# A decoder block's MLP: the down projection from seven block products instead of eight

## The chip, the cores and the metric

The kernel runs on one core of one Trainium2 chip. The metric is the device time of one execution in microseconds (us). The core's engines run side by side, each with its own instruction queue that it works off in order: TensorE (PE; its weight loads are shown apart as PEld), VectorE (DVE), ScalarE (ACT), GpSimd (POOL) and SyncE (SP), which here issues the transfers from HBM.

## What is computed

```python
# x: 256 tokens of 2048 channels, float32
xn = rmsnorm(x, norm_mix_pre);  proj = xn @ w_in          # mLSTM and attention branches, gates
x = x + rmsnorm(merged @ w_out, norm_mix_post)
hn = rmsnorm(x, norm_ffn_pre)
u = square(relu(hn @ w_up))                               # w_up:   2048 x 8192
y = u @ w_down                                            # w_down: 8192 x 2048
return x + rmsnorm(y, norm_ffn_post)
```

Only the last three lines, the MLP, are touched by the change (and where some tiles lie).

## The kernel before

Every weight is streamed once from HBM in units of 128 x 2048 float32 (1.05 MB). ScalarE casts a unit to float32r (`whi`), VectorE subtracts that from it (`wlo`), each in two halves of 1024 columns (`split`, L166 and L167). Three products then make one exact one: hi by hi, hi by lo, lo by hi. `whi` and `wlo` have four half-unit buffers each, so that a half can be split when PE is through with the half four places before it. `raw` units have three buffers.

The program is a list `steps` of (units, their products, what follows). The loop at its end splits the units of step i, then issues the products of step i - 1 and its follow-up, so a split is written one step ahead of its products. A scheduler in the build then sets the final order on each engine's queue; the engines keep to it.

The MLP works in `NCH` = 8 chunks of 1024 hidden channels.

- An *up step* (8 in a chunk) makes 128 channels of u for 256 tokens from one unit of w_up. `mm_feat` issues, for each of 16 k, one matmul of 512 columns (L185: the activation's hi and lo parts side by side) and one of 256 (L186). The two halves are then added by `both` (L216 copy on ScalarE, L218 on VectorE), scaled by `rbc`, squared with the relu (`up_post`, L726, L728), and split into hi and lo by `split_act` (L223, L224) into the tile `ut`.
- A *down step* (8 in a chunk: four column blocks `e` of 512, two halves `v` of the chunk's channels) takes one unit of w_down through `mm_tok`: 4 k, 2 token halves, 3 matmuls of 512 columns (L197, L201, L202), 24 in all. After `v` = 1 the sums of the two token halves are added into `y` in SBUF (L773; for the first chunk copied by ScalarE, L771).

Up steps of chunk j + 1 and down steps of chunk j follow each other eight by eight. The last chunk ends with `down_step` for two column blocks, `hold_step` (units split ahead) and `last_step`, which also does the last norm. The output projection's last unit alone goes through `mm_feat_one` (L209 to L211), three matmuls of 256 columns into one region.

```python
for k in range(KT):                       # mm_feat_one, the three of one k
    PE.matmul(out=acc[:, 0:T], lhsT=hi, rhs=m[:, 0, :], start=k == 0, stop=False)
    PE.matmul(out=acc[:, 0:T], lhsT=hi, rhs=m[:, 1, :], start=False, stop=False)
    PE.matmul(out=acc[:, 0:T], lhsT=lo, rhs=m[:, 0, :], start=False, stop=k == KT - 1)
```

Of the kernel before, what the change touches and what calls it, by code (L numbers as in the profile page):

```python
# [23 lines left out]
P = 128  # L24
# [8 lines left out]
# columns of the groups of av and the gates, and where they start  # L33
# [22 lines left out]
# 2 pi in three parts of 12 bits and a rest, for an exact reduction  # L56
# [29 lines left out]
def tile_hybrid_block(ctx, tc, xT, pos, pre, small, wa, wi, wo, wu, wd, wpost, out):  # L86
# [7 lines left out]
    pa = ctx.enter_context(tc.tile_pool(name="pa", bufs=1))  # L94
    pb = ctx.enter_context(ExitStack())
# [40 lines left out]
    def keep_warm(n):  # L136
        """Products that nobody reads, so that the tensor engine's clock is up."""
# [39 lines left out]
    def mm_feat(accs, units, mov, k0=0, nk=KT, after_k=None, tail=0):  # L177
        """The halves of accs[i][c, 512] sum to unit i's product; mov(k) is [128, 2, T]: hi, lo."""
# [11 lines left out]
    def mm_tok(accs, parts, mov, kbase, start, stop, halves=(0, 1), n=512):  # L190
        """accs[h][tok, n] accumulate over the unit's four k."""
# [12 lines left out]
    def mm_feat_one(acc, parts, mov):  # L204
        """acc[c, :T] is the product, in one region."""
        for k in range(KT):
            m = mov(k)
            hi, lo = wk(parts, k, P)
            PE.matmul(out=acc[:, 0:T], lhsT=hi, rhs=m[:, 0, :], start=k == 0, stop=False)  # L209
            PE.matmul(out=acc[:, 0:T], lhsT=hi, rhs=m[:, 1, :], start=False, stop=False)  # L210
            PE.matmul(out=acc[:, 0:T], lhsT=lo, rhs=m[:, 0, :], start=False, stop=k == KT - 1)  # L211

    def both(acc):
        """The two halves of mm_feat's result, added."""
# [6 lines left out]
    def split_act(dst, src, scale):  # L221
        """dst[:, 0], dst[:, 1] = hi, lo of src * scale (a number or one per partition)."""
# [4 lines left out]
    def newton(dst, y, v, n):  # L227
        """One step of dst = v ** -0.5 from y."""
# [5 lines left out]
    def rsqrt(dst, v, n):  # L234
        """dst = v ** -0.5, from the exponent's halving: no activation table is touched."""
# [8 lines left out]
    def rsqrt_act(dst, v, n):  # L244
        """dst = v ** -0.5 with a square root of the scalar engine and a step of Newton's."""
# [6 lines left out]
    def col_stats(col, sq, root):  # L252
        """col[tok, half] = rstd from the sums over channels of the arrays sq[channel, token]."""
# [11 lines left out]
    def bc_row(dst, col):  # L265
        """dst[any, tok] = col[tok]."""
# [24 lines left out]
    def rope_tables():  # L291
# [14 lines left out]
        # sin(ang) and sin(ang + pi/2), both arguments brought into [-pi, pi]  # L306
# [70 lines left out]
    def gates(pg):  # L377
# [13 lines left out]
        # log sigmoid(f) = min(f, 0) - log(1 + exp(-|f|))  # L391
# [9 lines left out]
        # with r = i - b: m - b per token (m0, and m1 - b's last sum of the first chunk; m1)  # L401
# [19 lines left out]
    def conv(cb, dst, acc):  # L421
# [11 lines left out]
        # twice silu(o) = o (1 + tanh(o / 2))  # L433
# [11 lines left out]
    def mlstm(h, qk):  # L445
# [16 lines left out]
        # q and k hold twice their values: 1/4 of that, and k's 256 ** -0.5  # L462
# [30 lines left out]
    def mlstm_out(h, hn):  # L493
        for vt in range(2):
# [5 lines left out]
            # times twice the sigmoid, 1 + tanh; the half follows  # L500
# [11 lines left out]
    def feat_step(src, mov, post, after_k=None, tail=0):  # L512
        st = {}

        def mm(units):
            st["a"] = [acc_tile() for _ in units]
            mm_feat(st["a"], units, mov, after_k=after_k, tail=tail)
# [40 lines left out]
    def gate_post(name, acc):  # L558
        s = both(acc)
        V.tensor_tensor(out=s, in0=s, in1=rbc, op=ALU.mult)  # L560
        g = pa.tile([P, T], F32, name="gt", tag="gt", bufs=8)
# [40 lines left out]
    def then(f, *args):  # L602
        """f follows the last step, after what already does."""
# [32 lines left out]
        # a head's memory is read two steps after its last unit  # L636
# [10 lines left out]
    def mix_post(c, acc):  # L647
# [6 lines left out]
        if c == 0:  # L654
            # the table of the square root, before it is waited for
# [15 lines left out]
    def residual():  # L671
        """x += mix's norm, and its operands for the MLP, in this order on the vector engine."""
# [32 lines left out]
    def open_mlp():  # L705
        """The residual by tokens."""
        pb.close()
        pool["f"] = pb.enter_context(tc.tile_pool(name="pf", bufs=1))
        x1 = late["x1"] = pa.tile([P, 2, D], F32, name="x1", tag="ha")
        late["y"] = pa.tile([P, 2, D], F32, name="y", tag="hm")  # L710
        late["wp"] = pool["f"].tile([P, D], F32, name="wp_bc")
        nc.sync.dma_start(out=late["wp"], in_=wpost.partition_broadcast(P))
        late["ssq"] = pool["f"].tile([P, 2, 4], F32, name="ssq")
        for k0 in range(0, KT, 4):
            for h in range(2):
# [4 lines left out]
                S.copy(out=x1[:, h, k0 * P:(k0 + 4) * P], in_=ps)  # L720

    ut = {}

    def up_post(j, i, acc):
        s = both(acc)
        V.tensor_tensor(out=s, in0=s, in1=rbc, op=ALU.mult)  # L726
        r = t256()
        V.scalar_tensor_tensor(out=r, in0=s, scalar=0.0, in1=s, op0=ALU.max, op1=ALU.mult)  # L728
        if i % 4 == 0:
            ut[j, i // 4] = pool["f"].tile([P, 4, 2, T], F32R, name="ut", tag="ut", bufs=4)  # L730
# [26 lines left out]

    def down_step(j, e, v):
        def mm(units):
            if v == 0:  # L760
                tok_acc["d"] = [acc_tile(), acc_tile()]
            mm_tok(tok_acc["d"], units[0], umov(j), 4 * v, v == 0, v == 1)

        def post():
            if v == 0:
                return
            y = late["y"]
            es = slice(e * 512, (e + 1) * 512)
            for h in range(2):
                if j == 0:  # L770
                    S.copy(out=y[:, h, es], in_=tok_acc["d"][h])  # L771
                elif j < NCH - 1:
                    V.tensor_tensor(out=y[:, h, es], in0=tok_acc["d"][h], in1=y[:, h, es],  # L773
                                    op=ALU.add)
                else:
                    last_sum(h, e, tok_acc["d"][h])
                    last_scale(h, e)
        steps.append(([wd[8 * j + 2 * e + v]], mm, post))

    def umov(j):  # L780
        return lambda k: ut[j, k // 4][:, k % 4]

    def last_sum(h, e, acc):
        """y's last part, and the sum of its squares."""
        y = late["y"][:, h, e * 512:(e + 1) * 512]
        add = V.tensor_tensor(out=y, in0=acc, in1=y, op=ALU.add)
        q = pool["f"].tile([P, 512], F32, name="q512", tag="q512", bufs=1)
# [3 lines left out]
    def last_scale(h, e):  # L791
        es = slice(e * 512, (e + 1) * 512)
# [3 lines left out]
    def hold_step(v):  # L796
        """A unit of the last step, split ahead of it into the place of the MLP's operands."""
# [8 lines left out]
    def last_step():  # L806
        """The last columns of y, the first tokens' before the others', and the last norm."""
        j, e = NCH - 1, 3

        def mm(units):  # L810
            units = late["held"] + units
            late["acc"] = [[acc_tile(), acc_tile()] for _ in range(2)]
            for h in range(2):
                for n in range(2):
                    for v in range(2):
                        mm_tok(late["acc"][n], units[2 * n + v], umov(j), 4 * v, v == 0, v == 1,
                               halves=(h,))

        def post():
# [3 lines left out]
            for h in range(2):  # L823
# [7 lines left out]
                yw = pool["f"].tile([P, 512], F32, name=f"yw{h}")  # L831
# [12 lines left out]
    for j in range(NCH + 1):  # L844
# [131 lines left out]
```

## Time and profile before

| | |
|---|---|
| runs shown | 1458.02, 1458.87, 1461.2 us; median 1458.87 |
| span of the profiled execution (first to last instruction) | 1456.0 us |
| that execution's own time | not listed; the median stands 2.87 us above the span |
| PE, PEld, DVE, ACT, POOL busy | 99%, 85%, 67%, 50%, 0% of the span |
| HBM read | 263.46 MB, 182 GB/s over the span |

Busy is the time in which an engine has at least one instruction in work. Matmuls are pipelined: a row's duration is longer than the distance to the next one's start, so the cost of a matmul is read from starts. An idle time is followed by what ended it. The clock row gives the granted TensorE clock in tenths of full speed.

### The profile page before, as it was taken

To read this page: it belongs to the slowest core of one execution; us is meant where nothing else is said; L and a number is where in the kernel's file an instruction comes from. 1 tells how busy PE (TensorE), PEld (TensorE's weight loads), DVE (VectorE), ACT (ScalarE), POOL (GpSimd) and SP (SyncE) were. 2 spreads that over 40 slices of the span, in tenths; PEclk is the share of its full clock that TensorE was granted. 3 is DMA by queue.
4 is the path that set the end of the run, shared out by engine and by line. 5 is a ranking of instruction groups with operands and counts; after the bars stand their busy time and mean duration, and the time that the engine had idled before them with its cause. 6 is when DMAs were issued, how large, how long until landed. Compare 5 with 4: busy or idle time off the path is not lost.

```text
span 1456.0 us, 19843 instructions
## 1 busy us (share of the span) xinstructions
PE 1444.0 (99%) x7722; PEld 1235.7 (85%) x7722; DVE 975.4 (67%) x1546; ACT 724.3 (50%) x1125; POOL 2.4 (0%) x12
## 2 busy tenths in 40 slices
PE   9999999999999999999999999999999999999997
PEld 8888888888888888888888888888888888888885
DVE  8777766686676666665778646566575665656675
ACT  7655555565554444555655444344343444434451
POOL 0000000000000000000000000000000000000000
PEclk9999999999999999999999999999999999999999
DMA  8554445555445555555634555555555555555561
GB/s 265 211 183 166 167 173 174 174 174 174 172 175 193 183 190 186 188 188 184 221 145 153 194 181 195 182 194 181 194 178 198 178 198 178 199 178 198 177 227 58
DMA packets 42141, 266.83 MB, mean 183 GB/s; under 512 B 4800, under 2 KB 7104, under 8 KB 11200
## 3 DMA queue, kind: packets, MB, share of 16 engines
q1 hardware_dynamic: 41904, 265.57, 52.4%
q8 instruction: 60, 0.98, 0.3%
q14 instruction: 33, 0.27, 0.1%
q10 hardware_dynamic: 144, 0.01, 0.0%
HBM read 263.46 MB, written 2.10 MB: 182 GB/s over the span
## 4 chain that ended last, share of the span: by engine, by line
PE 98%; ACT 1%; DVE 0%; DMA 0%; issue 0%; DVEq 0%; SPq 0%; ACTq 0%
PE acc L185 42%; PE acc L186 22%; PE acc L202 10%; PE acc L197 10%; PE acc L201 10%; PE sm L141 0%; PE sm L340 0%; ACT whi L166 0%; PE sm L457 0%; PE sm L364 0%; PE sm L447 0%; DMA raw<-in_wa_dram 0%; PE sm L359 0%; ACT x L720 0%; DVE x L839 0%
## 5 line engine op out<-in xcount | busy, mean ns | idle before, releaser
L167 DVE TENSOR_TENSOR wlo<-raw,whi 128x1024 fp32r<-128x1024 f32 (+2 forms) x504 | 599.9, 1191 | 422.6 <-ACT whi L166 412.8
L166 ACT CAST whi<-raw 128x1024 fp32r<-128x1024 f32 (+2 forms) x504 | 515.0, 1023 | 650.6 <-PE acc L185 296.6
L185 PE MATMUL acc<-xw,whi 128*128 128x512 f32 x1152 | 408.9, 395 | 0.0
L185 PE MATMUL acc<-hw,whi 128*128 128x512 f32 x992 | 349.8, 394 | 0.1
L186 PE MATMUL acc<-xw,wlo 128*128 128x256 f32 x1152 | 328.5, 285 | 0.0
L186 PE MATMUL acc<-hw,wlo 128*128 128x256 f32 x992 | 280.4, 283 | 0.0
L185 PEld LDWEIGHTS acc<-xw,whi 128*128 128x128 f32 x1152 | 216.4, 188 | 50.3 <-issue 2.1
L185 PEld LDWEIGHTS acc<-hw,whi 128*128 128x128 f32 x992 | 186.2, 188 | 43.2 <-DVE t L218 0.4
L186 PEld LDWEIGHTS acc<-xw,wlo 128*128 128x128 f32 x1152 | 216.7, 188 | 0.9
L202 PE MATMUL acc<-wlo,ut 128*128 128x512 f32 x496 | 197.6, 398 | 0.0
L201 PE MATMUL acc<-whi,ut 128*128 128x512 f32 x496 | 195.3, 394 | 0.0
L197 PE MATMUL acc<-whi,ut 128*128 128x512 f32 x496 | 194.9, 393 | 0.0
L186 PEld LDWEIGHTS acc<-hw,wlo 128*128 128x128 f32 x992 | 186.5, 188 | 0.4
L201 PEld LDWEIGHTS acc<-whi,ut 128*128 128x128 f32 x496 | 93.1, 188 | 23.6
L197 PEld LDWEIGHTS acc<-whi,ut 128*128 128x128 f32 x496 | 93.1, 188 | 22.1
L202 PEld LDWEIGHTS acc<-wlo,ut 128*128 128x128 f32 x496 | 93.1, 188 | 21.8
L185 PE MATMUL acc<-mg,whi 128*128 128x512 f32 x240 | 84.2, 393 | 0.0
L218 DVE TENSOR_TENSOR t<-acc,t 128x256 f32<-128x256 f32 x183 | 75.8, 417 | 0.9 <-ACT t L216 0.9
L186 PE MATMUL acc<-mg,wlo 128*128 128x256 f32 x240 | 67.7, 283 | 0.0
L216 ACT COPY t<-acc 128x256 f32<-128x256 f32 x183 | 66.6, 366 | 0.0
L197 PE MATMUL acc<-whi,xw 128*128 128x512 f32 (+1 forms) x160 | 54.4, 356 | 0.3 <-ACT whi L166 0.3
L201 PE MATMUL acc<-whi,xw 128*128 128x512 f32 (+1 forms) x160 | 54.6, 357 | 0.0
(234 smaller groups left out, 1238.4 us busy)
## 6 DMA issues: line engine op xcount, KB each, us to landing
raw<-in_wi_dram SPq DMA_DIRECT2D x96, 1024.0 KB, 4.8
raw<-in_wu_dram SPq DMA_DIRECT2D x64, 1024.0 KB, 4.9
raw<-in_wd_dram SPq DMA_DIRECT2D x64, 1024.0 KB, 4.8
raw<-in_wo_dram SPq DMA_DIRECT2D x16, 1024.0 KB, 4.8
raw<-in_wa_dram SPq DMA_DIRECT2D x8, 520.0 KB, 4.8
raw<-in_wa_dram SPq DMA_DIRECT2D x16, 256.0 KB, 4.7
x<-in_xT_dram SPq DMA_DIRECT2D x16, 128.0 KB, 4.6
out_dram<-x SPq DMA_DIRECT2D x8, 256.0 KB, 2.7
```

What stands on the lines that cost most here:

```text
L166: S.copy(out=hi[:, s], in_=r)
L167: V.tensor_tensor(out=lo[:, s], in0=r, in1=hi[:, s].bitcast(F32), op=ALU.subtract)
L185: PE.matmul(out=accs[i][:, 0:2 * T], lhsT=hi, rhs=m, start=k == 0, stop=False)
L186: PE.matmul(out=accs[i][:, 0:T], lhsT=lo, rhs=m[:, 0, :], start=False, stop=k == nk - 1)
L197: first = PE.matmul(out=acc, lhsT=m[:, 0, ts], rhs=hi, start=start and k == 0, stop=False)
L201: PE.matmul(out=acc, lhsT=m[:, 1, ts], rhs=hi, start=False, stop=False)
L202: PE.matmul(out=acc, lhsT=m[:, 0, ts], rhs=lo, start=False, stop=stop and k == 3)
L216: S.copy(out=b, in_=acc[:, T:2 * T])
L218: V.tensor_tensor(out=s, in0=acc[:, 0:T], in1=b, op=ALU.add)
```

## The change

For chunks 0 to 6 the down projection's block products (two token halves by two column blocks, summed over two channel halves) are made by a seven-product scheme in the manner of Strassen and Winograd. With A the chunk's activations (A11, A12: first token half, channel halves 0 and 1; A21, A22: second) and B the four weight units of a pair of column blocks, the steps of a group are, in program order:

| step | activation factor | weight factor | how the weight factor is made | goes into |
|---|---|---|---|---|
| p1 | A11 | B11 | loaded | v, and on to p2's bank |
| q5 | A21 - A22 | T1 = B11 + B12 | VectorE (L856) | y22, on to q3's bank |
| p6 | q5's - A11 | T2 = T1 + B22 | VectorE (L862), in place | v |
| p2 | A12 | B21 | loaded | with p1: y11 |
| q7 | A11 - A21 | T3 = B12 + B22 | accumulating transfer from POOL (L871) onto B12 | y22, on to q4's bank |
| q3 | p6's + A12 | B22 | loaded | with q5: y12 |
| q4 | A22 | T4 = T2 + B21 | VectorE (L878), in place | with q7: y21 |

The scheme's common sum `v` is kept over all chunks and added to y12, y21, y22 at the end of chunk 6. A chunk has two groups (column blocks 0 and 1, 2 and 3), so 14 *down steps*, each of 12 matmuls (`mm_factor`). The 8 up steps of the next chunk, U0 to U7, stand among them: p1 U0 q5 U1 p6 p2 U2 q7 U3 q3 q4 U4, then p1 U5 q5 p6 U6 p2 U7 q7 q3 q4. All up steps go through `mm_feat_one`; `up_post` is one operation on VectorE (L757) and a square on ScalarE; the seven activation factors of a chunk are split once (`factor`, L773 and L774). B22 is fetched twice. The last chunk keeps its ordinary steps. Line numbers of the changed kernel: L169 and L170 are the split, L215 to L217 an up step's matmuls, L226, L230, L232 a down step's, L846 and L897 the operations into v and y. Some tiles move (`x` and the gates into a pool that is closed for the MLP, `wp_bc` into a weight buffer near the end).

```diff
-    def mm_feat_one(acc, parts, mov):
+    def mm_feat_one(accs, units, mov, after_k=None, tail=0):
...
+    def mm_factor(acc, parts, f, start, stop, pinned=False, more=False):
+        for k in range(4):
+            hi, lo = wk(parts, k, 512)
+            first = PE.matmul(out=acc, lhsT=f[:, k, 0], rhs=hi, start=start and k == 0,
+                              stop=False, skip_group_check=more)
...
+            PE.matmul(out=acc, lhsT=f[:, k, 1], rhs=hi, start=False, stop=False,
+                      skip_group_check=more)
+            PE.matmul(out=acc, lhsT=f[:, k, 0], rhs=lo, start=False, stop=stop and k == 3,
+                      skip_group_check=more)
...
     def up_post(j, i, acc):
-        s = both(acc)
-        V.tensor_tensor(out=s, in0=s, in1=rbc, op=ALU.mult)
         r = t256()
-        V.scalar_tensor_tensor(out=r, in0=s, scalar=0.0, in1=s, op0=ALU.max, op1=ALU.mult)
+        V.scalar_tensor_tensor(out=r, in0=acc[:, 0:T], scalar=0.0, in1=rbc, op0=ALU.max,
+                               op1=ALU.mult)
...
-        split_act(ut[j, i // 4][:, i % 4], r, 1.0)
+        S.activation(out=uh[c][:, i % 4], in_=r, func=AF.Square)
+        if j < NCH - 1 and i == 7:
+            todo.extend(factors(j))
+            for _ in range(4):
+                todo.pop(0)()
...
+    def factor(name, src):
+        f = xs[name] = pool["f"].tile([P, 4, 2, P], F32R, name="xs", tag="xs", bufs=7)
+        S.copy(out=f[:, :, 0], in_=src)
+        V.tensor_tensor(out=f[:, :, 1], in0=src, in1=f[:, :, 0].bitcast(F32), op=ALU.subtract)
...
+    def long_raw():
+        return pool["f"].tile([P, 2048], F32, name="rawl", tag="rawl", bufs=4)
...
+        def w_t1():
+            r["12"], r["t"] = long_raw(), long_raw()
+            nc.sync.dma_start(out=r["12"], in_=b12)
+            V.tensor_tensor(out=r["t"], in0=r["11"], in1=r["12"], op=ALU.add)
+            return [split(r["t"])]
...
+        def w_t2():
+            r["22"] = long_raw()
+            nc.sync.dma_start(out=r["22"], in_=b22)
+            V.tensor_tensor(out=r["t"], in0=r["t"], in1=r["22"], op=ALU.add)
+            return [split(r["t"])]
...
+        def w_t3():
+            nc.gpsimd.dma_start(out=r["12"], in_=b22, accum_op=ALU.add)
+            return [split(r["12"])]
...
+        def w_t4():
+            V.tensor_tensor(out=r["t"], in0=r["t"], in1=r["21"], op=ALU.add)
+            return [split(r["t"])]
...
+    for j in range(NCH - 1):
+        downs, i = down_group(j, 0) + down_group(j, 1), 0
+        for what in "DUDUDDUDUDDUDUDDUDUDDD":
+            if what == "D":
+                steps.append(downs.pop(0))
+            else:
+                up_step(j + 1, i)
+                i += 1
```

What the build makes of this order shows on VectorE's queue. First the queue of the kernel before, where the down steps of a chunk end and the next chunk's up steps begin (`wlo` is a lo part of a half unit, `y` the output's sums, `t` an up step's temporary):

```order
L773 TENSOR_TENSOR y<-acc,y 128x512 x2
L167 TENSOR_TENSOR wlo<-raw,whi 128x1024 x3
L218 TENSOR_TENSOR t_9879<-acc,t_9877 128x256
L726 TENSOR_TENSOR t_9879<-t_9879,rbc 128x256
L728 SCALAR_TENSOR_TENSOR t_9882<-t_9879 128x256
L167 TENSOR_TENSOR wlo<-raw,whi 128x1024
L224 SCALAR_TENSOR_TENSOR ut<-t_9882,ut 128x256
```

Now the change's queue at the like place, from the operation on U7's sums (first row) into the steps q7, q3, q4 and p1 (`rawl`: weight buffers of the group; `s_a`, `s_b`, `u`: activations and their combinations; `xs`: a factor's lo part):

```order
L757 SCALAR_TENSOR_TENSOR t_10288<-acc,rbc 128x256
L170 TENSOR_TENSOR wlo<-rawl,whi 128x1024 x2
L897 TENSOR_TENSOR y<-y,acc 128x512
L784 TENSOR_TENSOR s_a<-u 128x512
L170 TENSOR_TENSOR wlo<-rawl,whi 128x1024
L170 TENSOR_TENSOR wlo<-raw,whi 128x1024
L846 TENSOR_TENSOR y<-y,acc 128x512
L789 TENSOR_TENSOR s_b<-s_a,u 128x512
L793 TENSOR_TENSOR u<-u 128x4x128
L170 TENSOR_TENSOR wlo<-raw,whi 128x1024
L774 TENSOR_TENSOR xs<-s_a,xs 128x4x128
```

Between the lo parts there now stand operations into y and on activation factors. Two up steps further on, from the operation on U1's sums (first row) to the lo parts of U2 and q7, the queue of the change is:

```order
L757 SCALAR_TENSOR_TENSOR t_10558<-acc,rbc 128x256
L170 TENSOR_TENSOR wlo<-rawl,whi 128x1024 x3
L878 TENSOR_TENSOR rawl<-rawl 128x2048
L170 TENSOR_TENSOR wlo<-raw,whi 128x1024
L846 TENSOR_TENSOR v<-v,acc 128x512
L170 TENSOR_TENSOR wlo<-raw,whi 128x1024
L170 TENSOR_TENSOR wlo<-rawl,whi 128x1024
```

The sum T4 (L878) stands ahead of U2's first lo part (the single L170 behind it). On PE's queue at the same place, the end of p2 (`acc_10395`) and the start of U2 (`acc_10617`) read:

```order
L232 MATMUL acc_10395<-wlo_10568,xs_10304 128x512
L226 MATMUL acc_10395<-whi_10567,xs_10304 128x512
L230 MATMUL acc_10395<-whi_10567,xs_10304 128x512
L232 MATMUL acc_10395<-wlo_10568,xs_10304 128x512
L226 MATMUL acc_10679<-whi_10609,xs_10330 128x512
L230 MATMUL acc_10679<-whi_10609,xs_10330 128x512
L217 MATMUL acc_10617<-hw_7141,wlo_10588 128x256
```

Two hi products of q7 (`acc_10679`), and further ahead two of U2, stand before U2's first lo product (L217).

## Rows read from the trace of the kernel before

**Rows 1.** Page, part 1 (busy us, share, instructions), part 2's clock

```profile
PE 1444.0 (99%) x7722; PEld 1235.7 (85%) x7722; DVE 975.4 (67%) x1546; ACT 724.3 (50%) x1125; POOL 2.4 (0%) x12
...
PEclk9999999999999999999999999999999999999999
```

**Rows 2.** Page, part 4: the chain that ended last, by engine and by line

```profile
PE 98%; ACT 1%; DVE 0%; DMA 0%; issue 0%; DVEq 0%; SPq 0%; ACTq 0%
PE acc L185 42%; PE acc L186 22%; PE acc L202 10%; PE acc L197 10%; PE acc L201 10%; PE sm L141 0%; PE sm L340 0%; ACT whi L166 0%; PE sm L457 0%; PE sm L364 0%; PE sm L447 0%; DMA raw<-in_wa_dram 0%; PE sm L359 0%; ACT x L720 0%; DVE x L839 0%
```

**Rows 3.** Windows: length; busy PE, PEld, DVE, ACT, POOL; clock; DMA share; GB/s

```profile
1100.00:1200.00 100.00, 100.00 (x494) 83.69 (x493) 62.48 (x78) 41.74 (x52) 0.00 (x0) 1.00 0.54 187
1400.00:1456.00 56.00, 46.53 (x200) 37.10 (x198) 34.72 (x53) 17.71 (x30) 0.00 (x0) 0.96 0.35 129
```

**Rows 4.** Line L197 (down products), its instructions from 818 and 1086 us

```profile
L197 PE MATMUL acc<-whi,ut x1: 400/400/400, 818.4 to 818.4; 128*128 128x512 f32 x1
...
L197 PE MATMUL acc<-whi,ut x3: 388/392/392, 1087.6 to 1089.0; 128*128 128x512 f32 x3
```

**Rows 5.** Timeline of PE, a stretch of down products (start us, us)

```profile
818.66 0.39 PE L201 MATMUL acc<-whi,ut 128*128 128x512 f32 x1
...
848.07 0.39 PE L201 MATMUL acc<-whi,ut 128*128 128x512 f32 x1
```

**Rows 6.** Timeline of PE, a stretch of up products

```profile
800.04 0.28 PE L186 MATMUL acc<-hw,wlo 128*128 128x256 f32 x1
...
818.30 0.28 PE L186 MATMUL acc<-hw,wlo 128*128 128x256 f32 x1
```

**Rows 7.** Timeline of PE, the output projection's last unit

```profile
709.25 0.28 PE L211 MATMUL acc<-mg,wlo 128*128 128x256 f32 x1
...
714.59 0.28 PE L211 MATMUL acc<-mg,wlo 128*128 128x256 f32 x1
```

**Rows 8.** Groups of VectorE by form (busy us, mean ns | idle before)

```profile
L167 DVE TENSOR_TENSOR wlo<-raw,whi 128x1024 fp32r<-128x1024 f32 x472 | 578.1, 1225 | 419.7 <-ACT whi L166 410.1 <-PE acc L186 7.8
...
L773 DVE TENSOR_TENSOR y<-acc,y 128x512 f32<-128x512 f32 x48 | 33.1, 691 | 0.7
L728 DVE SCALAR_TENSOR_TENSOR t<-t 128x256 f32<-128x256 f32 x64 | 27.2, 425 | 2.1
...
L167 DVE TENSOR_TENSOR wlo<-raw,whi 128x512 fp32r<-128x512 f32 x16 | 11.0, 688 | 1.6 <-ACT whi L166 1.6
```

**Rows 9.** Timeline of VectorE, at three places (xN: N merged)

```profile
736.17 1.22 DVE L167 TENSOR_TENSOR wlo<-raw,whi 128x1024 fp32r<-128x1024 f32 x1
737.30 0.47 DVE L688 SCALAR_TENSOR_TENSOR hw<-x,sm_in,hw 128x256 fp32r<-128x256 f32 x1
...
1019.77 1.39 DVE L773 TENSOR_TENSOR y<-acc,y 128x512 f32<-128x512 f32 x2
...
1426.14 1.28 DVE L794 TENSOR_TENSOR y<-y,wp_bc 128x512 f32<-128x512 f32 x2
```

**Rows 10.** Groups of ScalarE by line and form

```profile
L166 ACT CAST whi<-raw 128x1024 fp32r<-128x1024 f32 x472 | 495.6, 1050 | 640.4 <-PE acc L185 296.6 <-PE acc L201 189.8 <-issue 139.4
...
L788 ACT ACTIVATE q<-y 128x512 f32<-128x512 f32 x8 | 5.1, 633 | 18.4 <-DVE y L786 18.3
```

**Rows 11.** Timelines of ScalarE and VectorE, one half unit's split

```profile
1023.03 1.05 ACT L166 CAST whi<-raw 128x1024 fp32r<-128x1024 f32 x1 [1.75 <-PE acc L201]
...
1024.12 1.23 DVE L167 TENSOR_TENSOR wlo<-raw,whi 128x1024 fp32r<-128x1024 f32 x1 [1.57 <-ACT whi L166]
```

**Rows 12.** Waits, longest first (us in total, times, longest us)

```profile
DVE wlo L167 <- ACT whi L166: 412.8, 410, 3.8
ACT whi L166 <- PE acc L185: 296.6, 217, 4.9
```

**Rows 13.** Page, part 2 (GB/s by slice) and part 6 (KB, us to landing)

```profile
GB/s 265 211 183 166 167 173 174 174 174 174 172 175 193 183 190 186 188 188 184 221 145 153 194 181 195 182 194 181 194 178 198 178 198 178 199 178 198 177 227 58
...
raw<-in_wd_dram SPq DMA_DIRECT2D x64, 1024.0 KB, 4.8
```

More of the change, by code (lines that the diff above doesn't have):

```diff
@@ L729, in up_post @@
         if i % 4 == 0:
[L730 to L731 removed]
+            uh[c] = pool["f"].tile([P, 4, T], F32, name="u", tag="u", bufs=2)
+        S.activation(out=uh[c][:, i % 4], in_=r, func=AF.Square)
[3 more added lines that the diff above has]
+                todo.pop(0)()
+        elif j == NCH - 1 and i % 4 == 3:
+            for h in range(2):
+                factor((j, c, h), uh[c][:, :, h * P:(h + 1) * P])
@@ L756, in hmov, with wd_unit, group, add @@
         return late["hw"][:, k]
+    def wd_unit(j, e, v):
+        return wd[8 * j + 2 * e + v]
+    def long_raw():
+        return pool["f"].tile([P, 2048], F32, name="rawl", tag="rawl", bufs=4)
+    def group(j, p):
+        e1, e2 = 2 * p, 2 * p + 1
+        b11, b12, b21, b22 = (wd_unit(j, e, v) for v in range(2) for e in (e1, e2))
+        y, v = late["y"], late["v"][:, p]
+        y11, y12, y21, y22 = (y[:, h, e * 512:(e + 1) * 512] for h in range(2) for e in (e1, e2))
+        r, acc = {}, {}
+        def add(dst, a, op=ALU.add):
+            if j == 0 and op == ALU.add and id(dst) not in seen:
+                seen.add(id(dst))
+                S.copy(out=dst, in_=a)
+            else:
+                V.tensor_tensor(out=dst, in0=dst, in1=a, op=op)
+        seen = set()
+        def w_b11():
+            r["11"] = load(b11)
+            return [split(r["11"])]
+        def w_t1():
[8 more added lines that the diff above has]
+            return [split(r["t"])]
+        def w_b21():
+            r["21"] = long_raw()
+            nc.sync.dma_start(out=r["21"], in_=b21)
+            return [split(r["21"])]
+        def w_t3():
+            nc.gpsimd.dma_start(out=r["12"], in_=b22, accum_op=ALU.add)
+            return [split(r["12"])]
+        def w_b22():
+            return [split(r["22"])]
+        def w_t4():
+            V.tensor_tensor(out=r["t"], in0=r["t"], in1=r["21"], op=ALU.add)
+            return [split(r["t"])]
+        def step(name, w, bank, start, post):
+            def mm(units):
+                if start:
+                    acc[bank] = acc_tile()
+                mm_factor(acc[bank], units[0], xs[j, name], start, True, more=not start)
+            def after():
+                post(acc[bank])
+                if todo:
+                    todo.pop(0)()
+                if j == NCH - 2 and name == "q4":
+                    for dst, op in ((y12, ALU.subtract), (y21, ALU.add), (y22, ALU.subtract)):
+                        V.tensor_tensor(out=dst, in0=dst, in1=v, op=op)
+            return w, mm, after
+        def q7(a):
+            V.tensor_tensor(out=y22, in0=y22, in1=a, op=ALU.subtract)
+        return [step("p1", w_b11, "a", True, lambda a: add(v, a)),
+                step("q5", w_t1, "e", True, lambda a: add(y22, a)),
+                step("p6", w_t2, "f", True, lambda a: add(v, a)),
+                step("p2", w_b21, "a", False, lambda a: add(y11, a)),
+                step("q7", w_t3, "b", True, q7),
+                step("q3", w_b22, "e", False, lambda a: add(y12, a)),
+                step("q4", w_t4, "b", False, lambda a: add(y21, a))]
@@ L761, in mm @@
                 tok_acc["d"] = [acc_tile(), acc_tile()]
-            mm_tok(tok_acc["d"], units[0], umov(j), 4 * v, v == 0, v == 1)
+            for h in range(2):
+                mm_factor(tok_acc["d"][h], units[0], xs[j, v, h], v == 0, v == 1)
         def post():
[L765 to L775, printed above, removed]
+            if v == 1:
+                for h in range(2):
                     last_sum(h, e, tok_acc["d"][h])
                     last_scale(h, e)
-        steps.append(([wd[8 * j + 2 * e + v]], mm, post))
-    def umov(j):
-        return lambda k: ut[j, k // 4][:, k % 4]
+        steps.append(([wd_unit(j, e, v)], mm, post))
     def last_sum(h, e, acc):
@@ L791, in last_scale @@
     def last_scale(h, e):
+        if "wp" not in late:
+            late["wp"] = long_raw()
+            nc.sync.dma_start(out=late["wp"], in_=wpost.partition_broadcast(P))
         es = slice(e * 512, (e + 1) * 512)
```

118 lines of the change are left out of this document (80 added, 38 removed).

## The prediction

> **What bounds the kernel now.** I read the page's busy times first, then the chain, then the windows by stage. TensorE is busy 1444.0 of 1456.0 us, VectorE 975.4, ScalarE 724.3, and the granted clock is 1.0 (the upper level, 2.4 GHz) in every slice of the page [rows 1]. A busy PE is no proof of a full one, so the chain decides: 98% of it is PE, by the matmul lines of the two kinds of product [rows 2]. In 100 us of the MLP, PE is busy all the time, VectorE 62 us and ScalarE 42 us, with the DMA engines at 0.54 [rows 3]. The waits say the same: VectorE's lo parts wait for ScalarE's hi parts, and those for PE, which has to give the split buffers back [rows 12]. So fewer products save time, as long as VectorE keeps up. A chunk (8 up units, 8 down units) takes (1087.6 - 818.4) / 3 = 89.7 us [rows 4].
>
> **Products taken away.** A group of 2 by 2 blocks was 4 units of 24 matmuls; now it is 7 steps of 12. That is 12 fewer, in 14 groups 168. The 512-column matmuls of the down steps start (848.07 - 818.66) / 126 = 0.2334 us apart (43 rows of L201, every third matmul) [rows 5]: 168 x 0.2334 = **-39.2 us**. A down step is now 2.80 us.
>
> **The up units' third matmul.** 64 units of 16 k go from 512 + 256 columns to 3 x 256. The pair takes 18.26 / 52 = 0.3512 us [rows 6]. The three-matmul form already runs, in the output projection's last unit: 5.34 / 15 = 0.3560 us [rows 7]. 64 x 16 x 0.0048 = **+4.9 us**; an up step is 5.70 us. The Trainium skill (TensorE: Matmul & The Clock Gate, Part 3: Packing small matmuls) says that a weight load overlaps matmuls in flight only where the row group differs, and under LDWEIGHTS that 128 columns take 107 ns; 1024 bare loads would then add 110 us. By that rule the kernel would be slower by over 70 us; rows 7 speak against it, since a full load goes with each of those matmuls at 0.119 us.
>
> **VectorE's load.** Up steps lose three of four operations, but 22 weight units are now split per chunk where 16 were. Alone, an operation takes 1.225 us on 1024 columns, 0.69 on 512, 0.42 on 256 [rows 8]. Where VectorE has work queued the next one starts before the last ends: 1.13 to 1.14 us for 1024, 1.28 - 0.69 = 0.59 for 512; a 512 read from PSUM directly after another gave 1.39 - 0.69 = 0.70 [rows 9]. I take 1.14, 0.60, and 0.33 for 256 (0.42 less the same 0.09). A sum of 2048 columns is not in the trace: between twice a 1024 (2.45) and 1.225 + 2 x (1.225 - 0.688) = 2.30 alone; queued 2.21, which I take, as it is the straight line through the two lengths. The Trainium skill (VectorE: DVE Perf Modes, The TRN2 errata) has 2.29 us for it alone, against my 2.30; by it the sum would stay as it is. Per chunk: 44 half splits x 1.14 = 50.2, 6 weight sums x 2.21 = 13.3, 25 operations of 512 (11 on activation factors, 14 into y and v) x 0.60 = 15.0, 8 x 0.33 = 2.6: **81.1 us**, against 14 x 2.80 + 8 x 5.70 = **84.8 us** of PE. It fits by 4%, so the order decides.
>
> **Where PE will stall.** Read VectorE's queue from the end of U7 to U2's first half, the longest stretch rich in down steps. PE needs q7, q3, q4, p1, U0, q5, U1, p6, p2: 7 down steps (19.6) and 2 up steps (11.4), 31.0 us, and it has 0.7 us more of high products queued ahead of U2's first lo product (PE's queue in the section on the change). VectorE's queue holds, behind the operation on U7's sums and up to that lo part: 16 half splits (18.2), 15 operations of 512 (9.0), T2 and T4 (4.4), the operations on U0 and U1 (0.7) = 32.3 us. It can't start at once: q3's second half needs a buffer that U7 frees with its last matmul, and from cast to lo part is 1.09 us [rows 11], so it starts 1.25 after U7; p1's first half waits 0.25 more for q3's buffer. 32.3 + 1.5 = 33.8, so PE stands 33.8 - 31.7 = **2.1 us** in front of U2 or, in pieces, of U1 and p6. Elsewhere the same count leaves no stall: between U2 and U5 VectorE has 3 us over, from U5 to U7 it is nearly even (11 x 1.14 + 2 x 2.21 + 3 x 0.60 + 2 x 0.33 = 19.4 against 3 x 2.80 + 2 x 5.70 = 19.8), and lateness there is taken up by the wait for q3's buffer. The floor is 0 per chunk (the chain at under 31.7, if the wait for q3's half went beside other work); the ceiling takes every operation at its duration alone: 16 x 1.225 + 15 x 0.69 + 4.6 + 0.8 + 1.5 = 36.9, a stall of 5.2. I take 2.1, since rows 9 show the overlap wherever operations queue. Behind each late lo part stand the operations into y, which nobody waits for at once: the sums have five PSUM banks. Chunk 0 has fewer operations into y but all factors in a shorter stretch; I give it the same. 7 x 2.1 = **+14.7 us**.
>
> **What I cost at nothing.** ScalarE: 44 casts x 1.05 + 7 x 0.63 + 8 of half that length at no more than 0.63 = 56 us of 87 [rows 10]; its casts lie beside PE as before, and without that cover each would add its 1.05 us. Traffic: 18 units of 1.05 MB in 87 us is 217 GB/s, where 187 takes 0.54 of the DMA engines [rows 3]; the first slice of the page moved 265 [rows 13]. SP's queue: a plain load lands in 4.8 us [rows 13]. The tightest is the second block's load for the next first sum: its place comes free with p2's split, four half splits, one 512 and one 256 (5.5 us) before VectorE reaches T1, so 0.7 us over; if late by up to 1 us the wait for q3's buffer hides it, beyond that all of VectorE's queue stands behind T1. The accumulating transfer is the only work of POOL there; it starts behind T1, and q7's cast wants it some 31 us later (first group) or 37 (second). It isn't in the trace: 4.8 us at least; reading, adding and writing back at three times that, behind two plain loads, 24 us. Both are covered. The end of the kernel (the last chunk's ordinary steps and the norm, where the clock row shows 0.96 [rows 3]) keeps its 24-matmul units; the norm's weights are now loaded late, but with 11 us of products ahead.
>
> **The sum.** 1456.0 - 39.2 + 4.9 + 14.7 = 1436.4 us of span. The median of the runs shown is 1458.87, 2.9 above the profiled span; with that, **1439.3 us**, 1.3% faster. Stall bounds 0 and 5.2 per chunk give 1424.6 and 1461.0.
>
> **Rivals.** *No stall* (PE-bound throughout): VectorE's waits go beside one another, 1424.6, perhaps to 1430. For it: 81.1 of 84.8 us. Against: the order is fixed, and four down steps in a row (q7, q3, q4, p1) carry most of the factor operations.
> *VectorE without overlap, slower*: every operation in the chain starts only when the one before is through. The place is the same, U7 to U2, and in it U5 to U7, which at 11 x 1.225 + 2 x 2.30 + 3 x 0.69 + 0.84 = 21.0 is 1.2 over PE and hands on 0.3. Then 5.5 us per chunk: 1456.0 - 39.2 + 4.9 + 38.5 + 2.9 = 1463.1, slower by 0.3%. It turns slower when the stall passes (39.2 - 4.9) / 7 = 4.9 us. For it: whole-chunk durations are 44 x 1.225 + 6 x 2.30 + 25 x 0.69 + 8 x 0.42 = 88.4, above PE's 84.8. Against: rows 9. The Trainium skill states this very rule (VectorE: DVE Perf Modes, The DRAIN you can't avoid: the next operation can't issue until the pipe is empty); the row at 736.17, whose successor starts 0.09 us before its end, speaks against it here.
> *The accumulating transfer comes late*: over 31 us after its issue, six times a plain load, PE stands in front of q7 by the rest, and ScalarE's casts behind q7's too; at 40 us that is 9 us in 7 chunks, 1439 + 63 = 1502. Nothing in the trace speaks for it, but nothing measures such a transfer either.
> *The change does less than it says*: not so in the program; the matmuls are 84 per group.
>
> **How the numbers follow.** The forecast (a stall of 1 to 3.5 us per chunk, 1432 to 1449) has 0.50; no stall 0.14; between forecast and no overlap (1449 to 1459) 0.13; VectorE without overlap 0.17; a late transfer 0.06. Leaving out the late transfer, the lower half of the no-stall case and the upper part of the no-overlap case, the range is 1427 to 1461. A measurement of this kernel tells 0.2% (2.9 us) from no change. Faster: 0.50 + 0.14 + 0.13, and a little of the no-overlap case would still be the same: 0.77 faster, 0.09 same, 0.14 slower.
>
> **What would show it.** Chunks of 86.9 us, between 84.8 (no stall) and 90. Three 256-column matmuls in 0.356 us. Idle of PE some 2 us per chunk, ahead of lo products of U1, p6 or U2, released by VectorE's L170, and none released by L871's transfer. VectorE busy over 90% of a chunk. I am wrong if PE stalls in other places (q7, or U3 to U7), if lo parts wait for loads, or if VectorE's queued 1024 takes 1.2 us.

## The result and the profile after

Four runs of the changed kernel took 1439.98 to 1443.25 us, median 1441.02, where the kernel before took 1458.88 beside it. The ratio is 0.9883, with a 95% interval of 0.987 to 0.9895: 1.2% faster. The profiled execution has a span of 1438.9 us, 17.1 less than before.

The page of the changed kernel, busy times (part 1), the chain by engine and by line (part 4), and the issues of weight loads in the MLP (part 6: count, KB, us to landing):

```profile
PE 1415.9 (98%) x8578; PEld 1253.8 (87%) x8578; DVE 1148.0 (80%) x1607; ACT 816.2 (57%) x1200; POOL 14.5 (1%) x26
...
PE 85%; DVE 11%; issue 2%; ACT 1%; DMA 1%; SPq 0%; DVEq 0%; ACTq 0%
...
raw<-in_wu_dram SPq DMA_DIRECT2D x64, 1024.0 KB, 6.2
rawl<-in_wd_dram SPq DMA_DIRECT2D x42, 1024.0 KB, 7.8
raw<-in_wd_dram SPq DMA_DIRECT2D x22, 1024.0 KB, 4.9
rawl<-in_wd_dram POOLq DMA_DIRECT2D x14, 1024.0 KB, 10.7
```

Beside [rows 1, 2] PE is busy 28.1 us less, VectorE 172.6 more, and the chain, 98% PE before, now runs over VectorE for 11% of the span. The last row is the accumulating transfer: 10.7 us, more than twice a plain load of [rows 13], and no wait in the trace is released by it. The plain loads have become slower too.

The period of a chunk is read from VectorE's timeline by an operation that runs once per chunk, L784:

```profile
942.81 0.68 DVE L784 TENSOR_TENSOR s_a<-u 128x512 f32<-128x512 f32 x1
...
1290.93 0.68 DVE L784 TENSOR_TENSOR s_a<-u 128x512 f32<-128x512 f32 x1
```

Four chunks lie between, so a chunk takes 348.12 / 4 = 87.03 us (89.7 before, [rows 4]; the forecast had 86.9). In a window of one chunk (length; busy PE, PEld, DVE, ACT, POOL; clock, DMA share, GB/s) VectorE is now nearly full, at 81.88 us:

```profile
1030.00:1117.00 87.00, 85.58 (x554) 77.01 (x553) 81.88 (x84) 51.34 (x60) 1.71 (x2) 1.00 0.63 218
```

VectorE's timeline from the operation on U7's sums to U2's first lo part, and PE's at the two places where it stands:

```profile
1026.46 0.42 DVE L757 SCALAR_TENSOR_TENSOR t<-acc,rbc 128x256 f32<-128x256 f32 x1
1026.80 1.22 DVE L170 TENSOR_TENSOR wlo<-rawl,whi 128x1024 fp32r<-128x1024 f32 x1
...
1055.88 2.28 DVE L878 TENSOR_TENSOR rawl<-rawl 128x2048 f32<-128x2048 f32 x1
1058.08 1.21 DVE L170 TENSOR_TENSOR wlo<-raw,whi 128x1024 fp32r<-128x1024 f32 x1
1059.22 0.67 DVE L846 TENSOR_TENSOR v<-v,acc 128x512 f32<-128x512 f32 x1
```

```profile
1035.92 0.39 PE L230 MATMUL acc<-whi,xs 128*128 128x512 f32 x1
1036.75 0.50 PE L226 MATMUL acc<-whi,xs 128*128 128x512 f32 x1 [0.44 <-ACT whi L169]
...
1057.98 0.39 PE L230 MATMUL acc<-whi,xs 128*128 128x512 f32 x1
1059.35 0.39 PE L217 MATMUL acc<-hw,wlo 128*128 128x256 f32 x1 [0.98 <-DVE wlo L170]
```

From 1026.80 to 1059.22 VectorE works for 32.4 us with hardly a gap; the forecast had 32.3. PE's starts at the first place are 0.83 apart where 0.23 is normal, at the second 1.37, and each next one is late by another 0.1: 0.7 and 1.2 us lost, and 2.1 in all with 0.2 at 1052.3. At the second the queue's T4 (L878) and U2's lo part come last, as forecast. At the first, a high product of q5 is queued ahead of p1's last lo products and waits for ScalarE. VectorE's queue has no gap up to U2's lo part, so this wait adds nothing to the 2.1 us; it only takes 0.7 of them earlier. Both places recur in each steady chunk.

### The profile page after: what moved, and what is told of

It is laid out like the page before. It is cut to its first block, busy times and chain, and to the rows that moved or that the text cites. A ratio compares the mean times of both kernels' runs of the same rounds, so it can differ in the third digit from the quotient of the medians.

```text
span 1438.9 us, 21795 instructions
## 1 busy us (share of the span) xinstructions
PE 1415.9 (98%) x8578; PEld 1253.8 (87%) x8578; DVE 1148.0 (80%) x1607; ACT 816.2 (57%) x1200; POOL 14.5 (1%) x26
## 4 chain that ended last, share of the span: by engine, by line
PE 85%; DVE 11%; issue 2%; ACT 1%; DMA 1%; SPq 0%; DVEq 0%; ACTq 0%
PE acc L188 27%; PE acc L189 14%; PE acc L217 7%; PE acc L215 7%; PE acc L216 7%; DVE wlo L170 6%; PE acc L232 5%; PE acc L226 5%; PE acc L230 5%; PE acc L200 2%; PE acc L205 2%; PE acc L204 2%; DVE xs L774 1%; DVE rawl L862 1%; ACT whi L169 1%
## 5 line engine op out<-in xcount | busy, mean ns | idle before, releaser
L169 ACT CAST whi<-raw 128x1024 fp32r<-128x1024 f32 (+2 forms) x420 | 425.3, 1017 | 420.1 <-PE acc L188 179.1
L170 DVE TENSOR_TENSOR wlo<-raw,whi 128x1024 fp32r<-128x1024 f32 (+2 forms) x420 | 495.0, 1181 | 208.4 <-ACT whi L169 198.0
L217 PE MATMUL acc<-hw,wlo 128*128 128x256 f32 x992 | 279.9, 283 | 4.9 <-DVE wlo L170 4.9
L216 PE MATMUL acc<-hw,whi 128*128 128x256 f32 x992 | 279.2, 282 | 0.0
L215 PE MATMUL acc<-hw,whi 128*128 128x256 f32 x992 | 277.7, 282 | 0.0
L169 ACT CAST whi<-rawl 128x1024 fp32r<-128x1024 f32 x168 | 173.5, 1048 | 116.8 <-PE acc L216 52.2
L170 DVE TENSOR_TENSOR wlo<-rawl,whi 128x1024 fp32r<-128x1024 f32 x168 | 201.8, 1218 | 8.4 <-ACT whi L169 6.5
L217 PEld LDWEIGHTS acc<-hw,wlo 128*128 128x128 f32 x992 | 186.9, 188 | 9.9 <-DVE wlo L170 7.3
L215 PEld LDWEIGHTS acc<-hw,whi 128*128 128x128 f32 x992 | 186.0, 188 | 4.6 <-DVE t L757 0.2
L216 PEld LDWEIGHTS acc<-hw,whi 128*128 128x128 f32 x992 | 186.8, 188 | 2.0
L226 PE MATMUL acc<-whi,xs 128*128 128x512 f32 x440 | 174.8, 397 | 2.9 <-ACT whi L169 2.9
L232 PE MATMUL acc<-wlo,xs 128*128 128x512 f32 x440 | 172.4, 397 | 1.8 <-DVE wlo L170 1.8
L230 PE MATMUL acc<-whi,xs 128*128 128x512 f32 x440 | 173.7, 395 | 0.0
L232 PEld LDWEIGHTS acc<-wlo,xs 128*128 128x128 f32 x440 | 82.6, 188 | 21.0 <-DVE wlo L170 4.5
L226 PEld LDWEIGHTS acc<-whi,xs 128*128 128x128 f32 x440 | 82.7, 188 | 20.7 <-ACT whi L169 6.0
L230 PEld LDWEIGHTS acc<-whi,xs 128*128 128x128 f32 x440 | 82.7, 188 | 18.1
## 6 DMA issues: line engine op xcount, KB each, us to landing
rawl<-in_wd_dram POOLq DMA_DIRECT2D x14, 1024.0 KB, 10.7
```

Source lines behind the costliest of these rows:

```text
L169: S.copy(out=hi[:, s], in_=r)
L170: V.tensor_tensor(out=lo[:, s], in0=r, in1=hi[:, s].bitcast(F32), op=ALU.subtract)
L215: PE.matmul(out=acc, lhsT=hi, rhs=m[:, 0, :], start=k == 0, stop=False)
L216: PE.matmul(out=acc, lhsT=hi, rhs=m[:, 1, :], start=False, stop=False)
L217: PE.matmul(out=acc, lhsT=lo, rhs=m[:, 0, :], start=False, stop=k == KT - 1)
L226: first = PE.matmul(out=acc, lhsT=f[:, k, 0], rhs=hi, start=start and k == 0, stop=False, skip_group_check=more)
```

## The experiments

Eleven kernels ran, each beside the kernel before. Theory A is that of the prediction: a chunk takes PE's work, and on top what VectorE's queue between U7 and U2 is longer than PE's. Chunk periods are again read from starts of L784 over four chunks.

### The up units alone

In the kernel before, this part of the change by itself:

```diff
-        s = both(acc)
-        V.tensor_tensor(out=s, in0=s, in1=rbc, op=ALU.mult)
         r = t256()
-        V.scalar_tensor_tensor(out=r, in0=s, scalar=0.0, in1=s, op0=ALU.max, op1=ALU.mult)
+        s = t256()
+        V.scalar_tensor_tensor(out=s, in0=acc[:, 0:T], scalar=0.0, in1=rbc, op0=ALU.max,
+                               op1=ALU.mult)
+        S.activation(out=r, in_=s, func=AF.Square)
...
+                          product=mm_feat_one)
...
```

> The kernel before with one part of the change alone: the 64 up units of the MLP as three 256-column matmuls per k into one region, and the shorter follow-up (one VectorE operation, a square on ScalarE); the down projection stays as it was. Theory A (the terms of the prediction): +4.9 us, 64 x 16 x 0.0048, so 1463.8 us. Rival (the shorter follow-up frees VectorE and so buys time): at or under 1458.9. Rival (three full weight loads per k cost extra): over 1470.

1466.42 us, 1.0055 (1.004 to 1.007) of before: slower by 8.1 us, not 4.9. The term was mis-sized. PE's timeline at the ends of one stretch of eight up units, first in the kernel before, then in this one, and this one's window:

```profile
863.23 0.39 PE L185 MATMUL acc<-hw,whi 128*128 128x512 f32 x1
...
908.16 0.39 PE L197 MATMUL acc<-whi,ut 128*128 128x512 f32 x1
```

```profile
865.08 0.28 PE L212 MATMUL acc<-hw,whi 128*128 128x256 f32 x1
...
911.15 0.40 PE L197 MATMUL acc<-whi,ut 128*128 128x512 f32 x1
```

```profile
865.00:911.00 46.00, 46.00 (x385) 45.96 (x384) 24.96 (x30) 22.47 (x32) 0.00 (x0) 1.00 0.51 184
```

44.93 us for 128 k is 0.3510 for a pair, 46.07 is 0.3599 for the three: 0.0089 apart, not 0.0048, times 1024 is 9.1. The triples of [rows 7] were not at fault by their number: in this kernel too the same unit of the output projection takes 0.356, and the stretch here takes 0.360 from its first triples on. So the step depends on the place; what in it makes the difference stays open. No wait is shown in the stretch, and PEld, the weight loads, is busy 45.96 of 46.00 us. That the loads are what holds the three matmuls at 0.120 us each was not tested, and a full PEld does not tell the two places apart: over the triples of [rows 7] it is busy 5.30 of 5.30 us (709.3 to 714.6) at 0.119 per matmul.

### The sum T3 on VectorE instead of the accumulating transfer

```diff
-            nc.gpsimd.dma_start(out=r["12"], in_=b22, accum_op=ALU.add)
+            V.tensor_tensor(out=r["12"], in0=r["12"], in1=r["22"], op=ALU.add)
```

> The changed kernel with T3 added by VectorE (2.21 us, twice per chunk) from the units already there, in place of the accumulating transfer. One of the two sums then stands in VectorE's queue between U7 and U2, the other after U4, where VectorE has some time over. Theory A (VectorE's queue from U7 to U2 sets the stall): 2.2 us more per chunk, chunks of 89.2, about 1456 us (1453 to 1458). Rival 1 (VectorE idles 5 us of a chunk, so 4.4 fit): 1441, no change. Rival 2 (VectorE is the bound all along): 4.4 more per chunk, 1472. Rival 3 (the accumulating transfer costs time by its traffic or its lateness): faster than 1441.

1458.31 us, 0.9998 (0.9988 to 1.0007) of before, 17 more than the changed kernel: the whole gain is gone. VectorE's timeline:

```profile
947.07 0.68 DVE L784 TENSOR_TENSOR s_a<-u 128x512 f32<-128x512 f32 x1
...
1305.75 0.68 DVE L784 TENSOR_TENSOR s_a<-u 128x512 f32<-128x512 f32 x1
```

Chunks of 89.67 us, 2.64 more where 2.2 were expected, and a time just over the expected range. So 4.4 us more on VectorE cost 2.6, nearer to the one sum in the critical stretch than to none (rival 1) or both (rival 2). In this execution the granted clock fell to 0.50 for 3.4 us at 1047.8; the chunk around it (1036.85 to 1126.21) took 89.36, no more than the others, so the clock does not explain the 2.64. In this order of steps the accumulating transfer is what lets the seven products pay; no other order was run without it.

### The sum T4 left out, and T4 by a second accumulating transfer

T4 left out:

```diff
-            V.tensor_tensor(out=r["t"], in0=r["t"], in1=r["21"], op=ALU.add)
```

T4 by a transfer:

```diff
-            V.tensor_tensor(out=r["t"], in0=r["t"], in1=r["21"], op=ALU.add)
+            nc.gpsimd.dma_start(out=r["t"], in_=b21, accum_op=ALU.add)
```

> The changed kernel with the sum T4 left out: q4 multiplies T2 as it stands, so y21 lacks a part. VectorE loses 2.21 us between U1 and U2's first lo part, and 2.21 more in the second group. Theory A: the stall of 2.1 us per chunk goes, or down to the 0.7 that PE waits for ScalarE's cast of q5's first half; chunks of 84.9 to 85.6, 1428 to 1433 us. Rival 1 (loads that come late, or ScalarE, set the pace): 1438 or more, chunks of 87.

> The changed kernel with T4 made by a second accumulating transfer (B21 once more from HBM onto T2, after T2's split) in place of VectorE's sum; the result is the same. Theory A: as with T4 left out, 1428 to 1433 us, if such a transfer is as hidden as T3's: it has from p6's split to q4's, some 25 us, where T3's took 10.7 from issue to landing. Rival (two accumulating transfers per group, 1.05 MB each, slow each other and the plain loads): over 3 us slower than with T4 left out, with casts of q4 or sums T1 waiting for transfers.

1433.51 us (ratio 0.9828, 0.9813 to 0.9843) and 1435.52 (0.9844, 0.9829 to 0.9858). VectorE's timeline with T4 left out, then with the transfer:

```profile
941.42 0.68 DVE L784 TENSOR_TENSOR s_a<-u 128x512 f32<-128x512 f32 x1
...
1285.00 0.68 DVE L784 TENSOR_TENSOR s_a<-u 128x512 f32<-128x512 f32 x1
```

```profile
940.85 0.69 DVE L784 TENSOR_TENSOR s_a<-u 128x512 f32<-128x512 f32 x1
...
1285.07 0.69 DVE L784 TENSOR_TENSOR s_a<-u 128x512 f32<-128x512 f32 x1
```

Chunks of 85.90 and 86.06. Taking 2.2 us off VectorE's queue in the stretch took 1.1 off the chunk; the wait ahead of U2 is gone. The transfer is nearly as good as no work at all: 0.2 us per chunk and 2.0 in all behind it, less than the 3 of the rival. Some 1.0 us per chunk stays, in pieces around q4 and p1, which the count of theory A does not have. So the chunks and both times lie over what was expected, the times by 0.5 and 2.5.

### The order of steps

U2 ahead of p6:

```diff
-        for what in "DUDUDDUDUDDUDUDDUDUDDD":
+        for what in "DUDUUDDUDDDUDUDDUDUDDD":
```

U7 behind q7:

```diff
-        for what in "DUDUDDUDUDDUDUDDUDUDDD":
+        for what in "DUDUDDUDUDDUDUDDUDDUDD":
```

> The changed kernel with one letter of the order string moved: U2 comes before p6 and p2, U3 before q7, so that PE has one up step more before VectorE must have T4 and p2's halves through. All work is the same. Theory A (the stall is the balance of VectorE's queue against PE's between U7 and U2): up to U2's first lo part VectorE has 24.9 us against PE's 26.1, up to U3's 36.4 against 37.4, so the 1.3 us ahead of U2 go; what is left is up to 1.0 us around q4 and p1, where PE waited for casts of ScalarE also with T4 left out. Chunks of 85.5 to 85.9, 1433 us (1430 to 1436). Rival (VectorE's whole load per chunk, which is unchanged, sets the period): 1441, chunks of 87.0.

> The changed kernel with U7 moved behind q7, so that three down steps stand in a row at the chunk's end and not four. All work is the same. Theory A: between U7 and U2 both queues lose q7 alone; VectorE has 14 half splits, 14 operations of 512, two sums and two of 256, 29.5 us, and 1.5 of waiting, 31.0, against PE's 28.9: again 2.1, so no change, 1441 us (1438 to 1444). Rival (four down steps in a row make the stall): most of it goes, 1431 us.

VectorE's timeline with U2 ahead of p6, then with U7 behind q7:

```profile
942.17 0.68 DVE L784 TENSOR_TENSOR s_a<-u 128x512 f32<-128x512 f32 x1
...
1287.57 0.69 DVE L784 TENSOR_TENSOR s_a<-u 128x512 f32<-128x512 f32 x1
```

```profile
944.55 0.69 DVE L784 TENSOR_TENSOR s_a<-u 128x512 f32<-128x512 f32 x1
...
1293.59 0.68 DVE L784 TENSOR_TENSOR s_a<-u 128x512 f32<-128x512 f32 x1
```

U2 ahead of p6: 1436.49 us (0.9848, 0.9833 to 0.9863), 4.5 less with the same work, chunks of 86.35; both are just over what was expected. The wait ahead of U2 is gone, that at q5's first product stays. U7 behind q7: 1439.46 us (0.9866, 0.9851 to 0.988), chunks of 87.26 in the steady part against 87.03, so the shorter row of down steps gives nothing there. The 1.6 us come from outside it: PE's lost time in the last q3 and q4 falls from 2.4 to 0.5, and the output projection, which has no part in the change, ends 0.8 earlier (715.04). What counts is the sum over the stretch, not four down steps in a row, and not VectorE's whole load.

### Combining, and the next limit

On top of T4's transfer: the order with U2 ahead of p6; or p2's factor one step later:

```diff
-            for _ in range(4):
+            for _ in range(3):
                 todo.pop(0)()
```

or B21 in a plain unit buffer, in the one order and in the other:

```diff
-            r["21"] = long_raw()
-            nc.sync.dma_start(out=r["21"], in_=b21)
+            r["21"] = load(b21)
```

> T4 by a second accumulating transfer and U2 before p6, both. Theory A: each alone ends the wait for VectorE ahead of U2, so together they give no more than either: the 1.0 us around q4 and p1 stay, 1433 to 1436 us. Rival (the gains add, each takes another part of the stall): 1428 or less.

> T4 by a second accumulating transfer, and p2's activation factor (a cast of 0.57 us on ScalarE, an operation of 0.60 on VectorE) one step later than the three that follow U7, and so each factor behind it. Theory A: the 1.0 us that PE still waits per chunk around q4 and p1 come from ScalarE's casts of factors ahead of those of weights; with one less there the wait falls by some 0.6, chunks of 85.3, 1431 us. Rival (the wait is the way of a half buffer from PE over ScalarE and VectorE back to PE, which no factor stands in): no change, 1435 us.

> T4 by a second accumulating transfer, and B21 loaded into one of the three plain unit buffers in place of one of the group's four, so that the next group's B12 finds a free buffer earlier. Theory B (formed on the last runs: with T4 gone from VectorE the next limit of a chunk is the load ahead of T1, then the 1.0 us of half buffers around q4 and p1): in the order as it is T1 waits for loads only where VectorE has time over, so no change against T4's transfer alone: 1434 to 1436 us. Rival (loads cost time here too): 1432 or less.

> The same, with U2 ahead of p6. That order with T4's transfer took 1440.7 us where either alone took 1435.5 and 1436.5, and T1 waited there for B12's load in each group, up to 1.9 us, behind it all of VectorE's queue. Theory B: with the buffer free earlier these waits go, and with them the 5 us: 1434 to 1437 us. Rival (the order itself, or the traffic of the second transfer, costs the time): 1440, no change.

T4's transfer with U2 ahead of p6 took 1440.72 us, worse than either alone: a miss for theory A. Waits of VectorE from 1030 to 1292 us (us in total, times, longest) with both, then with B21 in a plain buffer:

```profile
DVE rawl L856 <- DMA rawl<-in_wd_dram: 6.0, 6, 1.9
```

```profile
DVE rawl L856 <- DMA raw<-in_wd_dram: 4.3, 3, 1.5
```

With both, T1 waited for B12 in every group of this stretch, since that unit gets its buffer late. With B21 in a plain buffer that row is gone (the one left is of the other unit, in three of six groups), and the time is 1433.57 us (0.9827, 0.9812 to 0.9841), chunks of (1283.38 - 940.30) / 4 = 85.77: the load was the cause, as theory B had it.

```profile
940.30 0.69 DVE L784 TENSOR_TENSOR s_a<-u 128x512 f32<-128x512 f32 x1
...
1283.38 0.69 DVE L784 TENSOR_TENSOR s_a<-u 128x512 f32<-128x512 f32 x1
```

The same buffer without the order's change gave 1433.86 us (0.9829, 0.9813 to 0.9845), just under the expected range and 1.7 less than T4's transfer alone, where theory B had no change. These two beat the changed kernel by some 7 us, and no run that computes the same was faster.

p2's factor one step later gave 1435.14 us, no change: one factor's cast less on ScalarE there does not shorten what is left around q4 and p1. The way of a half buffer from PE over ScalarE and VectorE back may be what is left; no run tested it, and more half buffers were not tried, so this stays open.

### The old up products in the changed kernel

```diff
-        V.scalar_tensor_tensor(out=r, in0=acc[:, 0:T], scalar=0.0, in1=rbc, op0=ALU.max,
-                               op1=ALU.mult)
+        s = both(acc)
+        V.scalar_tensor_tensor(out=r, in0=s, scalar=0.0, in1=rbc, op0=ALU.max, op1=ALU.mult)
...
-        feat_step(wu[8 * j + i], hmov, lambda a: up_post(j, i, a), product=mm_feat_one)
+        feat_step(wu[8 * j + i], hmov, lambda a: up_post(j, i, a))
...
```

> The changed kernel with the up units' products as before (512 and 256 columns, the two halves added by ScalarE and VectorE): PE has 6.1 us less to do in all, VectorE one more operation of 256 columns per up unit, 0.33 us, 2.6 per chunk, ScalarE a copy. Theory A: between U7 and U2 VectorE gets 1.0 more and PE 0.2 less, so the stall grows by 1.2, and from U5 to U7, where the two were even, by up to 1.0; less 0.8 of PE's work, a chunk of 87.4 to 88.4: 1444 to 1451 us, slower than the changed kernel. Rival (PE's work sets the time): 1435 us.

1450.51 us (0.9945, 0.993 to 0.996), 9.5 more than the changed kernel though PE has less to do. VectorE's timeline at three starts of a chunk, then a window inside the first of the four chunks (as above, the clock is the third value from the end):

```profile
950.44 0.69 DVE L784 TENSOR_TENSOR s_a<-u 128x512 f32<-128x512 f32 x1
...
1040.13 0.68 DVE L784 TENSOR_TENSOR s_a<-u 128x512 f32<-128x512 f32 x1
...
1306.56 0.68 DVE L784 TENSOR_TENSOR s_a<-u 128x512 f32<-128x512 f32 x1
```

```profile
975.20:978.60 3.40, 3.40 (x11) 2.68 (x10) 3.40 (x4) 1.04 (x1) 0.00 (x0) 0.50 0.84 272
```

Over the four, a chunk takes (1306.56 - 950.44) / 4 = 89.03; but in the first, behind a wait of PE for L170 of 2.07 us, the granted clock fell to its lower level, 1.2 GHz, for 3.4 us, and that chunk took 89.69. The other three took 88.81, still over the expected 87.4 to 88.4. One operation of 0.33 us per up unit on VectorE, with a copy on ScalarE ahead of it that this run does not separate, outweighs 0.1 us of PE. The third matmul, which costs 8 us where VectorE has time, pays where it has none.

## Why the prediction was right

The forecast was 1439.3 us; 1441.02 was measured, and the span was 1438.9 where the sum gave 1436.4. So the sum was 2.5 us short and the time only 1.7: the 2.9 us added between span and time came from two different executions, while in the profiled one they lie 1.75 apart (1440.65 and 1438.9).

- **Products taken away, -39.2.** PE has 8578 matmuls, 7722 - 168 + 1024, so this count holds.
- **The third matmul, +4.9.** Mis-sized. Over some 140 triples between 1060 and 1160 us the mean step is 0.357 us against 0.3510 for a pair: 1024 x 0.006 = 6.1. The triples were slower than those of [rows 7] that stood for them. The rule of the Trainium skill on weight loads (TensorE: Matmul & The Clock Gate, Part 3: Packing small matmuls), by which the kernel would have lost over 70 us, is not borne out: alone, the three full loads per k cost 8.1 us. The same section of the Trainium skill also lets a load run ahead into a background weight buffer; no run here shows which way the loads took.
- **VectorE's load, 81.1 per chunk.** 81.9 was measured. The sum of 2048 columns, which no row showed, took 2.28 us alone and 2.20 queued (L878 at 1055.88, the next start at 1058.08), where 2.30 and 2.21 were taken.
- **The stall, 2.1 per chunk, +14.7.** Right in size, cause and end for the steady chunks: 2.1 in each of five, with VectorE's queue of 32.4 us without a gap between U7 and U2. Taking T4 from that stretch took 1.1 of the 2.1 away, putting PE's work into it 0.7; adding work to it lengthened the chunk. The forecast was wrong in three details. 0.7 of the stall shows as a wait for ScalarE at q5's first product, not for L170. Behind VectorE's queue stands a second limit of some 1.0 us around q4 and p1, which the forecast did not have; as VectorE's queue has no gap, it costs nothing in the changed kernel, and it shows when the queue is shortened. And the stall is not seven times the same: chunks 0 and 1 lost 0.8 and 1.1, and the last q3 and q4, which the forecast had at nothing, lost 2.4 (PE's timeline, below). 0.8 + 1.1 + 5 x 2.1 + 2.4 = 14.8 agrees with 14.7 in part by luck.

```profile
1381.20 0.50 PE L232 MATMUL acc<-wlo,xs 128*128 128x512 f32 x1 [1.29 <-DVE wlo L170]
...
1385.27 0.50 PE L232 MATMUL acc<-wlo,xs 128*128 128x512 f32 x1 [0.54 <-DVE wlo L170]
```

- **What was costed at nothing.** It held for the transfers: the accumulating one had 26 us in chunk 0 and over 30 later, and needed 10.7, 14.0 at most. The margin called tightest, B12's load ahead of T1, was indeed gone (T1 waits 0.25 us for it at 1023.12, hidden), and it became the limit when T4's transfer and U2's new place together had shortened VectorE's queue. The forecast did not name B11's load: T1 of a chunk's second group waits for it in every chunk, 0.2 to 1.5 us, also hidden, since VectorE has time over there. Not foreseen were 1.2 us in the kernel's first stretch, which the change doesn't touch: the output projection ends at 715.82 where it ended at 714.59 before. A wait of 0.92 for ScalarE at 11.29 is most of it; the same point varies from 714.3 to 716.2 over the kernels tried.

In sum, 1456.0 - 39.2 + 6.1 + 14.8 + 1.2 = 1438.9, the measured span.

Of the rivals, VectorE without overlap fell with the queue's 32.4 us: durations alone would give 35.4, the forecast's 36.9 less its 1.5 of waiting. (The 88.4 us given for it per chunk are 88.3 by their own terms.) The late transfer fell with its 10.7 us. The Trainium skill (VectorE: DVE Perf Modes, The DRAIN you can't avoid) has, beside the rule that the prediction took from it, an exception: a next operation that the page does not count as held starts earlier. The trace agrees with the exception: the operation behind L878 starts 0.08 before its end.

## What to carry to other kernels

When PE's work is cut, lay VectorE's queue and PE's side by side over each stretch between two points where they meet, at queued durations: a few us too many in one stretch cost time though the whole period has room. Such a stretch can be eased by taking work off the engine (two accumulating transfers per group did two sums; against leaving T4 out, the second cost 2.0 us in all), by one more matmul that saves the engine an operation, or by moving PE's work into it, which costs nothing; then look for the load or buffer that is next. Price a new form of matmul where it will stand: the same three took 0.356 in one place and 0.360 in another.

## What the runs showed of the hardware that was not expected

The step of three 256-column matmuls is not one number: 0.356 over [rows 7], 0.357 in the changed kernel, 0.360 over 128 k in a row, always at a granted clock of 1.0. An accumulating transfer of 1 MB takes 10.7 us to land (8.2 to 14.0); with two per group the median is 8.8. Plain loads beside it are about as slow: in the MLP, the 43 issued while one was in flight took 9.3 (median, 6.4 to 12.1), the 66 that met none 5.0, and with T3 on VectorE, where no transfer adds and two units fewer are read per chunk, plain loads took 4.8. What of this is the adding and what the traffic, no run separates; none has an accumulating transfer by itself. The Trainium skill (DMA: Bandwidth & Descriptors, Anatomy of one DMA — SWDGE (gpsimd) path) has a fit for transfers issued from GpSimd, 2.0 us plus their bytes at 436 GB/s, by which 1 MB would take about 4.4 us, an estimate. These rows are of transfers that also add, and take about twice that and more.

The granted clock fell to 0.50 for 3.4 us twice in the MLP with the old up products, and twice with T3 on VectorE, the two kernels where PE lost most time; in the first, 512-column matmuls then started 0.43 us apart instead of 0.23. In the changed kernel it stayed at 1.0 through the MLP.
